# Output projection of a hybrid decoder layer by pairs of token blocks, with seven products of sums for half of the features

## The chip, the cores and the metric

The kernel runs on one core of one Trainium2 chip. The time is the device time of one execution in microseconds (us); the profile adds one execution that was recorded by the hardware profiler. TensorE is called PE here (PEld is its loading of weights), VectorE is DVE, ScalarE is ACT, GpSimd is POOL, and SP is SyncE, which only issues transfers.

## What is computed

One layer for 4096 prompt tokens and 64 sample tokens of width 1024, all in float32:

```python
h = _rmsnorm(x, g_pre)
z = h @ w_in
cb, cc, ch, cg, q, k, v, ag, mq, mg = _split_cols(z)
out_a = jax.nn.silu(cg) * cb * conv          # 256 features, conv of width 3 over cc * ch
out_b = jax.nn.silu(ag) * o_b                # 512 features, attention in a window of 128, 8 heads, 2 kv heads, sinks
out_c = jax.nn.silu(mg) * o_c                # 256 features, attention into 256 memory tokens, 4 heads
y = jnp.concatenate([out_a, out_b, out_c], axis=-1) @ w_out
return x + _rmsnorm(y, g_post), new_conv, new_k, new_v
```

The last three lines matter most here: a concatenation `mix` of 1024 features per token, its product with the 1024 x 1024 matrix `w_out`, and the normalisation of that product's rows.

## The kernel before

A float32 product is made of three matmuls on rounded parts: every operand is split into a high part (a copy in the format `F32R`) and a low part (the rest), and high x high, low x high and high x low are added in a PSUM bank. In the code these are the triples `((0, 0), (1, 0), (0, 1))`.

The program has two large stages. `input_projection` makes z for all tokens in three phases (itself with Strassen's seven products) and stores queries, keys, values and gates in DRAM buffers `qd`, `vd`, `md`; near its end it also makes the memory keys and handles the first chunk's attention. Then `open_attention` opens the pools of the second stage, which runs over 32 blocks of 128 prompt tokens; two blocks are a chunk of 256 tokens, and `NCH` is 16 chunks.

A `Block` (line 1565) is one block's output projection. `load` fetches its rows of x into `xr` (two buffers), `split` makes the high and low parts of the block's `mix`, and `run` (line 1592) goes through two halves of 512 output columns; each half accumulates 8 k-steps of 128 features, three matmuls a step, in one bank of the PSUM pool `z`, which has two. After a half, DVE multiplies the bank by the gain `gpost` into `yn` (line 1614) and ACT squares the bank in place and sums the squares (line 1615). The row factor is made on DVE and POOL (lines 1620, 1621), and `finish` (line 1629) adds the scaled `yn` to `xr` and stores the result; it is called through `finish_block` in the next block.

The attention of two blocks ahead is woven into this. `starts_of` gives for each k-step the functions that are traced ahead of its matmuls; a number in `first_at`, `memory_at` and `second_at` is a k-step counted through all blocks, 16 to a block. For each half chunk h:

- `first_half` (line 1644): transposes of the memory probabilities of the half before, window scores of this half (line 1323), the products of probabilities and values of the half before (lines 1381, 1387, 1059), its gates, and this half's softmax. This is the burst of attention in the traces.
- `memory_half`: memory scores (line 1345) and their softmax.
- `second_half`: transposes of the window's probabilities (line 1369), their masks by POOL (lines 1302, 1305), and transposes of values.

The loads come by whole chunks: `chunk_load` fetches keys (`kst`, 384 positions, four DMAs from POOL's queue, line 1088), values and queries (`q`, six DMAs from SP's queue from chunk 2 on, line 1103); `load_mix` fetches the chunk's `mix` (three places in turn).

The order of PE's instructions is the order of the program up to block 25 (a manual schedule); from block 26 on PE, and on DVE, ACT, POOL and SP all through the second stage, the framework's scheduler sets the order when the program is built, apart from instructions pinned by `keep_in_program_order`. Each engine then goes through its own list in that order. The 64 sample tokens' attention is cut into pieces that `late` calls in blocks 26 to 30, and their output block stands between blocks 30 and 31; block 31 has its second half in two parts of 256 columns.

SBUF tiles of 4 KB a partition come from the pool `wa` of 21: 16 hold the split `w_out` (`wo[k][half]`), one holds `gpost`, four are left for the parts of `mix`.

## Time and profile before

| | |
|---|---|
| median of 3 runs | 1524.7 us (1523.94 to 1525.41) |
| profiled execution | 1525.19 us |
| its span in the trace | 1523.4 us |
| granted PE clock, mean | 0.999 |
| first output matmul starts | 929.9 us into the span |
| DMA in all | 306.31 MB |

The profile's page has, in this order, the busy time of each engine, the span in 40 slices, the DMA queues, the chain of work that ended last (followed back from the last instruction, at each step to what released it), the costliest groups of instructions, and the DMA issues. A row of a group names line, engine, operation, output and input; `x24` is the number of instructions, then come the busy time, the mean in ns of one, and after the second bar the engine's idle time just before them with what ended it. A timeline row starts with start and duration in us. A windows row has the stretch, its length, then busy time and number of instructions for PE, weight loads, DVE, ACT and POOL, the granted clock, the DMA share and GB/s. Matmuls are pipelined: a group's mean for one is longer than the distance between two.

### The profile page before, as it was taken

The page shows a single profiled execution, that of the slowest core. Times are in us where ns is not written, and L with a number is a line of the kernel's source. Part 1 is how long each engine was busy: PE and PEld are TensorE (multiplying, and loading weights), DVE is VectorE, ACT ScalarE, POOL GpSimd, SP SyncE. Part 2 cuts the span into 40 slices and gives each one's busy share as a digit, 9 for nine tenths or more (in the row PEclk, how much of TensorE's full clock was granted, in tenths as well). Part 3 has the DMA queues.
Part 4 walks back from the last instruction along what each step waited for, and adds up shares of the span by engine and source line. Part 5 has one row for each costly group of instructions (what it writes and reads, how often), then busy time and mean ns, then how long its engine had stood idle before and what let it go on. Part 6 is the DMA issues. An engine that isn't in the chain of part 4 may idle for free.

```text
span 1523.4 us, 30591 instructions
## 1 busy us (share of the span) xinstructions
PE 1511.3 (99%) x11581; PEld 1395.8 (92%) x11581; DVE 1137.1 (75%) x1965; ACT 794.3 (52%) x1949; POOL 334.3 (22%) x551
## 2 busy tenths in 40 slices
PE   9999999999999999999999999999999999999998
PEld 9999999999999999999999999888788888888877
DVE  6779887899988777896776768776666666666653
ACT  6676665575322222354454446566555555655541
POOL 0223322211300000000101302333433333444310
PEclk9999999999999999999999999999999999999999
DMA  9999999978855333578787797966665666666332
GB/s 271 165 242 228 283 287 270 267 243 297 209 182 182 127 127 115 192 230 283 237 262 242 210 304 250 272 157 169 164 150 149 156 156 162 154 150 152 129 122 97
DMA packets 178456, 306.31 MB, mean 201 GB/s; under 512 B 34438, under 2 KB 108166, under 8 KB 178278
## 3 DMA queue, kind: packets, MB, share of 16 engines
q1 hardware_dynamic: 153749, 249.41, 55.4%
q0 software_dynamic: 23840, 53.90, 14.3%
q8 instruction: 92, 1.51, 0.5%
q10 hardware_dynamic: 720, 1.05, 0.2%
q14 instruction: 55, 0.44, 0.1%
HBM read 197.23 MB, written 108.05 MB: 200 GB/s over the span
## 4 chain that ended last, share of the span: by engine, by line
PE 82%; DMA 8%; DVE 4%; issue 2%; ACT 2%; POOL 1%; SPq 0%; DVEq 0%; POOLq 0%; ACTq 0%
PE c L368 44%; PE y L1607 23%; PE ws L1323 3%; DMA nat<-in_x_p 2%; PE wo L1387 2%; PE wo L1059 2%; PE xs L1345 2%; PE xt L1357 2%; PE wt L1369 2%; PE wo L1381 1%; DMA x_0B<-in_xt 1%; DMA qd<-zh 1%; PE mem_acc L789 1%; DMA ws2A<-in_w_in 1%; DMA ws4A<-in_w_in 1%
## 5 line engine op out<-in xcount | busy, mean ns | idle before, releaser
L1607 PE MATMUL y<-wo,mh 128*128 128x512 f32 (+1 forms) x1040 | 341.6, 394 | 0.0
L375 DVE TENSOR_TENSOR z<-c,z 128x520 f32<-128x520 f32 (+1 forms) x308 | 194.6, 646 | 81.1 <-PE c L368 79.8
L1607 PEld LDWEIGHTS y<-wo,mh 128*128 128x128 f32 x1040 | 194.3, 188 | 44.2 <-issue 6.8
L1607 PE MATMUL y<-wo,ml 128*128 128x512 f32 (+1 forms) x520 | 201.8, 388 | 0.0
L1279 ACT ACTIVATE sm<-sm,wnm 128x128 f32<-128x128 f32 x256 | 99.5, 390 | 70.8 <-DVE wnm L1273 70.8
L1181 POOL TENSOR_SCALAR xp<-xp,xrd 128x256 f32<-128x256 f32 x128 | 60.5, 486 | 262.0 <-DVE xrd L1175 261.5
L1607 PEld LDWEIGHTS y<-wo,ml 128*128 128x128 f32 x520 | 97.9, 188 | 16.7
L1169 ACT ACTIVATE xp<-xs,xnm 128x256 f32<-128x256 f32 x128 | 59.1, 474 | 54.1 <-PE wt L1369 34.5
L1614 DVE TENSOR_TENSOR yn<-y,gpost 128x512 f32<-128x512 f32 (+1 forms) x66 | 45.1, 683 | 42.9 <-PE y L1607 42.5
L1305 POOL TENSOR_SCALAR_AFFINE_SELECT wpt<-wpt 128x512 f32<-128x512 f32 x64 | 59.3, 944 | 43.8 <-ACT wpt L1297 43.1
L1333 DVE COPY_PREDICATED sm<-wmask,ws 128x512 f32<-128x512 uint8 x60 | 40.6, 731 | 37.6 <-ACT sm L1332 37.6
L1088 POOL DMA_DIRECT2D kst<-qd x64 | 38.9, 624 | 105.6 <-PE ws L1323 82.7
L737 POOL CAST wmask<-negs 128x256 uint8<-128x256 f32 x1 | 1.1, 1113 | 266.9 <-DMA negs<-in_wmask 266.9
L1323 PE MATMUL ws<-kst,q 128*128 128x256 f32 (+1 forms) x480 | 55.8, 297 | 0.0
L276 ACT ACTIVATE nat<-nat 104x1024 f32<-104x1024 f32 x40 | 42.3, 1059 | 25.4 <-DMA nat<-in_x_p 25.4
L1615 ACT ACTIVATE y<-y 128x512 f32<-128x512 f32 (+1 forms) x66 | 38.2, 579 | 32.6 <-DVE yn L1614 32.6
L1361 ACT COPY xpt<-xt 128x512 f32<-128x512 f32 x30 | 17.6, 587 | 72.0 <-DVE xpt L1361 72.0
L407 ACT CAST zh<-z 128x520 fp32r<-128x520 f32 x56 | 33.4, 625 | 36.5 <-DVE z L375 32.4
L1323 PEld LDWEIGHTS ws<-kst,q 128*128 128x128 f32 (+1 forms) x480 | 46.5, 187 | 4.1
L377 ACT COPY z<-c 128x520 f32<-128x520 f32 (+1 forms) x44 | 24.4, 554 | 48.8 <-PE c L368 44.6
L1279 ACT ACTIVATION_READ_ACCUMULATOR sm<-sm,wnm 128x1 f32 x256 | 48.1, 188 | 0.0
L1629 DVE SCALAR_TENSOR_TENSOR xr<-yn,yst,xr 128x1024 f32<-128x1024 f32 (+2 forms) x34 | 43.1, 1269 | 5.6 <-POOL yst L1621 4.1
(973 smaller groups left out, 5069.8 us busy)
## 6 DMA issues: line engine op xcount, KB each, us to landing
q<-qd SPq DMA_DIRECT2D x84, 256.0 KB
xr<-in_x_p SPq DMA_DIRECT2D x32, 512.0 KB
nat<-in_x_p SPq DMA_DIRECT2D x39, 416.0 KB
o_yp<-xr SPq DMA_DIRECT2D x31, 512.0 KB
md<-th POOLq DMA_DIRECT2D x48, 260.0 KB, 6.4
qd<-zh SPq DMA_DIRECT2D x48, 260.0 KB
qd<-z SPq DMA_DIRECT2D x48, 260.0 KB
kst<-qd POOLq DMA_DIRECT2D x60, 192.0 KB, 4.1
```

Source lines behind the costliest of these rows:

```text
L276: S.activation(t[:RG], t[:RG], AF.Square, accum_out=r[:RG, i : i + 1])
L368: TE.matmul(bank[:, :HW], l, r, start=first and i == 0, stop=last and i == 3 * KH - 1)
L375: add = lambda dst, other: V.tensor_tensor(dst, c, other, op=ALU.add)
L1169: S.activation(p[:, i, :], s[:, i, :], AF.Exp, bias=nm[:, i : i + 1], scale=SCALE, accum_out=den[:, i : i + 1])
L1181: G.tensor_scalar(p[:, i, :], p[:, i, :], self.rds[h][:, i : i + 1], 0.5, op0=ALU.mult, op1=ALU.mult)
L1279: S.activation(sm[:, hh, :], sm[:, hh, :], AF.Exp, bias=nm[:, hh : hh + 1], scale=SCALE, accum_out=den[:, hh : hh + 1])
L1305: G.affine_select(p3, p3, pattern=[[0, 4], [1, P]], compare_op=ALU.is_ge, fill=0.0, base=0, channel_multiplier=-1)
L1323: TE.matmul(out(kvh, col, bank), q(kvh, col, bank)[r], k(kvh, part)[r], start=first, stop=True, skip_group_check=not first, **place)
L1333: V.copy_predicated(sm4, third["wmask"].unsqueeze(1).to_broadcast([P, 2, 2, P]), s4[:, :, :, 0:P])
L1607: TE.matmul(acc, self.hl[l][:, k], wo[k][c0 // 512][:, r, c0 % 512 : c0 % 512 + c1 - c0], start=j == 0, stop=j == passes * KT - 1)
L1614: V.tensor_tensor(yn[:m, c0:c1], acc[:m], gpost[:m, c0:c1], op=ALU.mult)
L1629: x = V.scalar_tensor_tensor(self.xr[:m, cs], yn[:m, cs], st[:m, 3:4], self.xr[:m, cs], op0=ALU.mult, op1=ALU.add)
```

## The change

Blocks 0 to 5 (chunks 0 to 2) go as before. From chunk 3 on, the two blocks of a chunk are one `Pair`. Its `mix` has 256 tokens and 1024 features; for the first 512 features (convolution and memory) tokens and features are cut in two, and the columns of `w_out` too, so that four products of quarters become Strassen's seven products of sums. The other 512 features (window attention) stay plain. The seven use five sums of parts of `w_out`, T1, T3, T4, T6 and T7, made once during the first six blocks (`weight_sum`; T6 and T7 go to DRAM and back, into slots of `wo` that are free by then), and for each pair four sums of parts of `mix`, made on POOL and split by ACT and DVE. Two accumulators are read in the middle of their sums (`s3`, `s4` and the differences), and later sums are added outside PSUM. The order of the products is that of `run`.

A pair has 30 k-steps; where the attention's functions stand changes with it. Queries and keys are loaded by half chunks (`half_load`, traced in `second_half`), keys with 256 positions for each half, and from chunk 2 on both from SP's queue. `mix` has two places instead of three, and `yn` two buffers instead of one. The memory probabilities' transposes are copied back into their own tile. The memory keys and values have tiles of their own. The sample block uses T3 and T4 too, 32 matmuls as before, and is run inside the last pair, whose last quarter is made in two halves of 256 columns. PE's manual order ends before chunk 13, as before at block 26.

```diff
-        vp = ctx.enter_context(tc.tile_pool(name="vp", bufs=5, side="right"))
+        vp = ctx.enter_context(tc.tile_pool(name="vp", bufs=4, side="right"))
...
+        wt = att.enter_context(tc.tile_pool(name="wt", bufs=6))
+        places = {tag: att.enter_context(tc.tile_pool(name=tag, bufs=2)) for tag in ("sm", "p", "yn", "pt", "pv")}
+        sums = {tag: att.enter_context(tc.tile_pool(name=tag, bufs=1)) for tag in ("s3", "s4", "sum")}
...
+        def load_keys(self, i):
+            t = self.t0 + i * P
+            pool = bp["k"] if i else third["pre"]
+            self.ks[i] = pool.tile([P, 4, P + CT] if i == 0 else [P, 4, CT], F32R, tag="k", name=f"kst{self.c}_{i}")[:, :, :CT]
+            self.fill_keys(G if self.c == 1 else DMA, self.ks[i], t - P, CT)
...
+        def load_queries(self, i):
+            self.q[i] = third["pre"].tile([P, 12, P], F32R, tag="q", name=f"q{self.c}_{i}", bufs=2)
...
-                pt = work([P, 2, CT], "xpt", f"xpt{c}_{2 * i + j}")
+                pt = self.xps[j]
...
+    class Pair:
+        def lows(self, t, src):
+            S.copy(t[:, 0], src)
+            V.tensor_tensor(t[:, 1], src, f(t[:, 0]), op=ALU.subtract)
...
+        def sums_of(self, raw, t, *terms):
+            raw = raw[:, : t.shape[2] * P].rearrange("p (b n) -> p b n", n=P)
+            n = t.shape[2] // len(terms)
+            for i, (x, y, op) in enumerate(terms):
+                G.tensor_tensor(raw[:, n * i : n * i + n], x, y, op=op)
+            self.lows(t, raw)
...
+            def product(acc, a, ws, new, cs=left_):
+                for k, w in enumerate(ws):
+                    if cs.start == 0:
+                        starts.get(at[0], lambda: None)()
+                        at[0] += 1
+                    for i, (l, r) in enumerate(((0, 0), (1, 0), (0, 1))):
+                        first = new and k + i == 0
+                        TE.matmul(acc, a[:, l, k], w[:, r, cs], start=first, stop=k == len(ws) - 1 and i == 2, skip_group_check=not new)
...
+            def done(n, p, acc):
+                cs = (left_, right_)[p]
+                V.tensor_tensor(y[n][:, cs], acc, gpost[:, cs], op=ALU.mult)
+                square(n, p, acc, acc)
+            def added(n, p, acc, s, junk, cs=None):
+                cs = cs or (left_, right_)[p]
+                V.tensor_tensor(y[n][:, cs], acc, s, op=ALU.add)
+                if n == 1:
+                    finish_block(True)
+                square(n, p, y[n][:, cs], junk)
+                self.blocks[n].factor(st[n])
+                G.tensor_tensor(y[n][:, cs], y[n][:, cs], gpost[:, cs], op=ALU.mult)
...
+            c12, c21 = psum("z", f"y{c}_c12"), psum("z", f"y{c}_c21")
+            product(c12, self.a11, t["T3"], True)
+            S.copy(s3, c12)
+            product(c21, self.a22, t["T4"], True)
+            S.copy(s4, c21)
+            product(c12, self.rows[0], b22, False)
+            V.tensor_tensor(y[0][:, left_], s3, c12, op=ALU.subtract)
+            G.tensor_tensor(y[0][:, left_], y[0][:, left_], s4, op=ALU.add)
+            product(c21, self.rows[1], b11, False)
+            less = sums["sum"].tile([P, 512], F32, tag="sum", name=f"less{c}")
+            V.tensor_tensor(less, s4, c21, op=ALU.subtract)
+            G.tensor_tensor(s3, s3, less, op=ALU.add)
+            product(c12, self.w[0], plain(1, range(4, 8)), False)
+            done(0, 1, c12)
+            product(c21, self.w[1], plain(0, (4, 5)), False)
+            c11 = psum("z", f"y{c}_c11")
+            product(c11, self.diagonal, t["T1"], True)
+            V.tensor_tensor(s3, s3, c11, op=ALU.add)
+            product(c21, self.w[1][:, :, 2:4], plain(0, (6, 7)), False)
+            done(1, 0, c21)
+            product(c11, self.down[1], t["T7"], False)
+            product(c11, self.w[0], plain(0, range(4, 8)), False)
+            added(0, 0, c11, y[0][:, left_], s4)
+            ends(0)
+            if not last:
+                c22 = psum("z", f"y{c}_c22")
+                product(c22, self.down[0], t["T6"], True)
+                product(c22, self.w[1], plain(1, range(4, 8)), False)
+                added(1, 1, c22, s3, s4)
+                ends(1)
+                return
...
+    def weight_sum(o, k):
+        t = wt.tile([P, 2, 512], F32R, tag="w", name=f"wt{o}{k}")
+        raw = [sums[tag].tile([P, 512], F32, tag=tag, name=f"w{tag}{o}{k}") for tag in ("s3", "s4")]
+        for r, (kk, h) in zip(raw, (x, y)):
+            DMA.dma_start(r, a["w_out"][kk + k][:, 512 * h : 512 * h + 512])
+        G.tensor_tensor(raw[0], raw[0], raw[1], op=op)
...
+    PLAIN_PAIRS = 3
+    start_of = lambda c: 32 * c if c < PLAIN_PAIRS else 32 * PLAIN_PAIRS + 30 * (c - PLAIN_PAIRS)
...
+    first_at = {2: 4, 3: 20, 4: 34, 5: 48, 6: 62, 7: 76, 8: 90}
+    first_at |= {h: start_of((h - 3) // 2) + 8 + 15 * ((h - 3) % 2) for h in range(9, 2 * NCH + 1)}
+    memory_at = {h: n + (7 if h == 2 else 5) for h, n in first_at.items()}
+    second_at = {h: n + (12 if h == 2 else 9 if h > 9 and h % 2 == 0 else 8) for h, n in first_at.items()}
...
+        at(e - 10, p.plain_parts)
+        at(e - 3, p.row_sums)
+        at(e - 2, lambda p=p: p.window_parts(0))
+        at(e + 2, lambda p=p: p.window_parts(1))
+        at(e + 4, p.diagonal_sum)
+        at(e + 8, p.column_differences)
+        at(start_of(c - 1) + 6, p.load)
```

In the names of the steps, step n of a pair is the n-th of its 30 k-steps: T3 has 0 and 1, T4 2 and 3, b22 4 and 5, b11 6 and 7, the window's part of c12 8 to 11, of c21 12, 13, 16 and 17, T1 14 and 15, T7 18 and 19, the window's part of c11 20 to 23, T6 24 and 25, and the window's part of c22 26 to 29.

361 lines of the change are left out of this document (235 added, 126 removed).

## The prediction

> **What bounds the kernel now.** I read the page's first part first, then its chain of waits, then the chain in order of time over two blocks in the middle of the output stage, then busy times of that stage.
>
> ```profile
> span 1523.4 us, 30591 instructions
> PE 1511.3 (99%) x11581; PEld 1395.8 (92%) x11581; DVE 1137.1 (75%) x1965; ACT 794.3 (52%) x1949; POOL 334.3 (22%) x551
> PE c L368 44%; PE y L1607 23%; PE ws L1323 3%; DMA nat<-in_x_p 2%; PE wo L1387 2%; PE wo L1059 2%; PE xs L1345 2%; PE xt L1357 2%; PE wt L1369 2%; PE wo L1381 1%; DMA x_0B<-in_xt 1%; DMA qd<-zh 1%; PE mem_acc L789 1%; DMA ws2A<-in_w_in 1%; DMA ws4A<-in_w_in 1%
> ```
>
> The profiled execution took 1525.2 us, 1.8 beside its span, 0.5 above the median of the runs shown (1524.7). PE is busy throughout, but a busy PE need not be a full one, so the chain in order of time decides (start, length, what):
>
> ```profile
> 1204.19 5.49 PE y L1607 x24
> 1209.68 0.87 PE xt L1357 x8
> 1210.55 1.62 PE ws L1323 x15
> ...
> 1214.65 4.30 PE y L1607 x18
> 1218.95 0.95 PE xs L1345 x8
> 1219.90 1.39 PE y L1607 x6
> 1221.29 0.87 PE wt L1369 x8
> 1222.16 0.22 PE vtp L1681 x2
> 1222.38 5.50 PE y L1607 x24
> ```
>
> Every piece is PE's, one behind the other: this stage lasts as long as its matmuls take to issue. 24 output matmuls take 5.49 us, 0.229 us each (the 389 ns of one in the groups include overlap). The block from 1204.19 to 1222.38 has 18.2 us: 48 x 0.229 = 11.0 of output and 7.2 of attention, 5.0 of it in one burst (1209.68 to 1214.65). The other engines have room here (PE clock 1.00, DMA share 0.61):
>
> ```profile
> 1100.00:1300.00 200.00, 200.00 (x1338) 164.81 (x1337) 134.88 (x310) 115.69 (x410) 77.30 (x122) 1.00 0.61 151
> 1199.31 0.34 SPq L1632 DMA_DIRECT2D o_yp<-xr  x1
> 1235.47 0.34 SPq L1632 DMA_DIRECT2D o_yp<-xr  x1
> ```
>
> (The stores are two rows of SP's timeline.) Columns of the first row: window, sum, then PE, weight load, DVE, ACT, POOL, clock, DMA. The two stores lie two blocks apart: 36.2 us. In these DVE works 134.88/200 x 36.2 = 24.4 us, ACT 20.9, POOL 14.0.
>
> **What the change removes.** Two blocks now cost 2 x 16 k-steps of three matmuls, 96. Counted from the calls of `product`, a pair costs seven products of two k-steps (42 matmuls; T3, T4, b22, b11, T1, T7, T6) and the window's sixteen k-steps left plain (48), 90. Thirteen pairs save 13 x 6 = 78 matmuls of 512 columns, 78 x 0.229 = **17.9 us**. The attention's matmuls stay as many, the sample block's 32 too. So 17.9 is all there can be; the rest is what is given back.
>
> **The load on the other engines, per pair.**
>
> ```profile
> L1332 ACT COPY sm<-ws 128x512 f32<-128x512 f32 x22 | 11.8, 589 | 0.8
> L1287 DVE TENSOR_TENSOR sm<-sm,wrd 128x512 f32<-128x512 f32 x22 | 15.2, 692 | 0.8
> L1614 DVE TENSOR_TENSOR yn<-y,gpost 128x512 f32<-128x512 f32 x22 | 15.1, 688 | 15.9 <-PE y L1607 15.9
> L1589 DVE TENSOR_TENSOR ml<-mix,mh 128x1024 fp32r<-128x1024 f32 x8 | 12.2, 1530 | 1.8 <-ACT mh L1588 1.8
> L1588 ACT CAST mh<-mix 128x1024 fp32r<-128x1024 f32 x7 | 7.4, 1054 | 1.9 <-PE y L1607 1.9
> L1398 DVE TENSOR_TENSOR mix<-mix,wo 128x256 f32<-128x256 f32 x7 | 2.9, 414 | 0.0
> ```
>
> DVE loses two L1589 (3.1) and four L1614 (2.8). It gains four 512-column and three 256-column low parts and seven 512-column operations on accumulators: 11 x 0.69 + 3 x 0.41 = 8.8. Net 2.9: 27.3 us in a pair of 36.2 - 1.4 = 34.8, 78%. ACT loses 2 x 1.05 and gains six 512-column copies (four parts, s3, s4) and three of half size: 6 x 0.59 + 3 x 0.4 - 2.1 = 2.6, to 23.5 (68%). POOL has no two-input operation of this width now; its sums, adds and gains by gpost come to 512 + 256 + 512 + 512 + 512 + 1024 = 3328 columns a pair.
>
> ```profile
> L1302 POOL TENSOR_SCALAR_AFFINE_SELECT wpv<-wpt x62: 627/636/1620, 850.1 to 1462.0; 128x512 f32<-128x512 f32 x62
> L468 POOL TENSOR_TENSOR cacc<-cacc,z x4: 323/388/460, 391.7 to 397.5; 128x64 f32<-128x64 f32 x4
> L1088 POOL DMA_DIRECT2D kst<-qd x20 | 12.1, 620 | 11.9 <-PE ws L1323 10.3 <-issue 1.6
> ```
>
> (Shortest, median and longest in the first two rows.) Bounds: one-input masks of 512 columns at a median of 636 ns (1.24 ns a column, 4.1 us a pair) and the narrow two-input add at 388 ns for 64 (6.1 ns a column, mostly its start, 20.2 us). I take 2.5 ns, twice the lower since two tensors are read: 8.3 us. The key loads' issues leave POOL (4 x 0.62): 14.0 - 2.5 + 8.3 = 19.8, 57%. No engine passes PE by its sum; what counts is when each hands over. [...]
>
> **The hand-overs, where PE can now wait.** There are two accumulators (`z`). Today 24 matmuls lie between the end of one use and the next need of its bank. In a pair the places are: step 4 needs s3's copy of c12 (steps 2, 3 between: 6 matmuls, 1.4 us, and a value/mask turn); step 6 needs s4 (1.4 us); step 8 needs y0's subtraction (1.4 us and a burst); step 12 needs `less`; step 14 takes c12's bank for c11, after `done` (gain on DVE, then square on ACT); step 18 needs s3's addition. ACT's copy takes 0.59 and DVE's operation 0.69, so a free engine keeps all of these. The tight one is step 14, as the same work is placed today at the same distance behind a burst:
>
> ```profile
> 1217.21 0.62 PE L1607 MATMUL y<-wo,mh 128*128 128x512 f32 x2
> 1218.38 0.68 DVE L1614 TENSOR_TENSOR yn<-y,gpost 128x512 f32<-128x512 f32 x1
> 1219.10 0.58 ACT L1615 ACTIVATE y<-y 128x512 f32<-128x512 f32 x1 [0.49 <-DVE yn L1614]
> ```
>
> The bank's last matmul ended by about 1217.4, DVE came 1.0 us later, because it was still in the softmax that follows the burst, and ACT let the bank go at 1219.7: 2.3 us. In a pair steps 12 and 13 (1.4 us) and the memory scores (0.95) lie between: 2.3 us. Nothing hides what comes on top. Lower bound 0. Upper bound: two of the new 0.69 operations (a low part, an addition) stand ahead, 1.4 us, and 0.2 of semaphores: 1.6 us a pair. I take 0.3 us, near the lower row, since `less`, y0 and the low parts fall due before or in the burst, in which DVE is mostly idle: 13 x 0.3 = **3.9 us** (0 to 21). Behind T1's waiting matmul stand the second half's transposes, for which ACT's mask copies and POOL's masks wait.
>
> From the memory scores at step 28 to step 6 of the next pair ACT has three part copies, s3, s4 and a square, 6 x 0.59 = 3.5 us, beside the exponentials and mask copies that it has there today, in eight steps (5.5 us) and the memory and value turns (0.95 + 0.87 + 0.22). It is full there, and a copy that stands one place too low costs its 0.59: I take **0.5 us** in all, 0 to 8 (0.6 a pair), near the lower end since the 1.4 us between use and use cover two such places.
>
> The masks on POOL follow the second half's transposes, and the next burst needs them:
>
> ```profile
> 1206.63 1.22 POOL L1302 TENSOR_SCALAR_AFFINE_SELECT wpv<-wpt 128x512 f32<-128x512 f32 x2
> 1207.81 2.20 POOL L1305 TENSOR_SCALAR_AFFINE_SELECT wpt<-wpt 128x512 f32<-128x512 f32 x2
> ...
> 1212.10 0.43 PE L1381 MATMUL wo<-wpv,vt 64*64 64x256 f32 x2
> ```
>
> They are done at 1210.0, needed at 1212.1: 2.1 us spare. The second half moves two steps closer to the burst (six instead of eight, 1.4 us), but the memory half moves as far ahead of it. Between them POOL gets the diagonal sum (256 columns, 0.6 us, in its idle time) and y0's addition (1.3): 0, with 2.1 us as cover.
>
> **Loads.** Keys go from POOL's queue to SP's, as eight loads a chunk instead of four and 2 x 256 positions instead of 384; queries as twelve of 512-byte rows instead of six of 1024.
>
> ```profile
> q1 hardware_dynamic: 18095, 26.10, 49.0%
> SPq L1632 <- DVE wden L1284: 181.7, 20, 14.0
> L1103 SPq DMA_DIRECT2D q<-qd x83: 573/611/746, 945.4 to 1386.7; - x83
> DMA to landing us min/median/max: 3.4/4.1/10.8
> ```
>
> (Queue totals of the same 200 us; SP's waits from 1000 to 1500: sum, times, longest; issue of the queries; landing of the keys.) A packet takes 0.49 x 16 x 200 / 18095 = 87 ns. A pair adds 1536 packets of queries and 512 of keys: at most 2048 x 87 ns / 16 = 11 us on each DMA engine, at least the bytes alone (0.25 MB, 1.7 us at 151 GB/s). The share goes from 0.61 to between 0.68 and 0.95. A half's ten issues take 6.1 us, landing 4.1 (the keys' row), and an output store waiting for DVE holds SP for 181.7/20 = 9.1 us: 19.3 in sum. From the second half in which the load is issued to the burst that reads it are 22 steps (15.1 us) and some 7 of attention: 22. Covered, by little; I take 0, upper end below.
>
> **First chunks and the end.** Ten weight sums, each two loads of 256 KB, one operation on POOL, ACT and DVE, and T6, T7 out and back, come while DMA is full:
>
> ```profile
> 940.00:960.00 20.00, 20.00 (x135) 16.55 (x135) 14.36 (x37) 12.98 (x52) 7.18 (x13) 1.00 1.12 282
> ...
> 1511.77 0.28 PE L1607 MATMUL y<-wo,ml 128*128 128x256 f32 x1
> ...
> 1517.29 0.28 PE L1607 MATMUL y<-wo,mh 128*128 128x256 f32 x1
> 1517.60 0.37 ACT L1615 ACTIVATE sq<-y 128x256 f32<-128x256 f32 x1 [1.88 <-PE y L1607]
> 1519.06 1.41 DVE L1629 SCALAR_TENSOR_TENSOR xr<-yn,yst,xr 128x512 f32<-128x512 f32 x2 [0.41 <-POOL yst L1621]
> ```
>
> (First the stretch from 940, with the columns of the window above and a DMA share of 1.12; then the timeline of the end.) PE runs unhindered in the stretch even so, and half chunks ask for less ahead: **0.6 us**, 0 to 5. At the end both kernels have matmuls of 256 columns, and 48 of them take 5.5 us, 0.115 each, half of 0.229: nothing. Behind the last one an addition of 256 columns (0.41) now precedes the square: **0.5 us**.
>
> Sum: 1525.2 - 17.9 + 3.9 + 0.5 + 0.6 + 0.5 = 1512.8 for the profiled execution, 1512.3 for the median. With the lower ends 1507; with all of the likely middle 1519.
>
> **The rivals.** *The banks eat it.* At 17.4/13 = 1.3 us of waiting a pair nothing is left. For it: DVE at 78% and a 2.3 us release against 2.3 us. Against: elsewhere in the pair bursts cover. At 1.3 us: 1525.2 - 17.9 + 16.9 + 1.6 - 0.5 = 1525.3.
>
> *Keys late on SP: slower.* For it: holds up to 14.0 us and landings to 10.8 make 30.9 against 22, 9 us late; POOL's own queue had no such hold. It decides from 3 us beyond the usual 19.3. If one half in three of 26 is 4 us late, some 9 x 4 = 36: 1548. Against: the waiting stores belong to steps 29 and 8, three steps and more ahead of the loads at 2 and 16.
>
> *POOL and DVE keep each other out.* The 636 ns mask takes up to 1620, L1589 spreads from 1215 to 1755 ns where both run. If each added operation is so blocked, by 1.0 us, diagonal sum and y0 take 0.6 + 1.3 + 2.0 = 3.9 ahead of the masks, 1.8 beyond the spare 2.1, in each pair: 23 us, 1535. The break-even is 3.5 us of POOL ahead of the masks.
>
> ```profile
> L1589 DVE TENSOR_TENSOR ml<-mix,mh x20: 1217/1500/1755, 958.3 to 1444.3; 128x1024 fp32r<-128x1024 f32 x20
> ```
>
> [...]
>
> *It doesn't do what it says*: the period is set elsewhere and PE only looks full. Then 1524.7. The chain speaks against it.
>
> **Chances.** Forecast 0.68 (its own range 1507 to 1519), banks 0.14, keys 0.07, POOL 0.08, nothing 0.03. What a measurement can tell from no change is about 0.2%, 3.0 us. Faster, under 1521.7: 0.68 and 0.05 of the banks, 0.73. Within: 0.06 of the banks and 0.03, 0.09. Slower: 0.07 + 0.08 + 0.03, 0.18. From 1506.5 to 1528 lie the forecast but for 0.02 and the banks but for 0.02, and nothing: 0.81.
>
> **What would show it.** In the profile after: 78 fewer matmuls, output matmuls 0.229 us apart; pairs some 35.1 us apart; gaps before T1's matmuls of a few tenths, none before the masks' consumers; DVE near 78%. It is wrong if PE waits over 1.3 us a pair, for DVE or ACT at T1 (banks), for a DMA at the window scores (keys), for POOL at the masks' products.

## The result, and the profile after

The changed kernel is slower: median 1574.3 us of four runs (1572.2 to 1577.4) against 1525.1 of the kernel before on the same chip, a ratio of 1.032 (95% interval 1.028 to 1.035). The forecast was 1512.3 with a range up to 1528. The profiled execution took 1572.2 us.

The first part of the page after the change, with the columns of before:

```profile
span 1570.3 us, 30978 instructions
PE 1518.9 (97%) x11497; PEld 1384.7 (88%) x11497; DVE 1195.0 (76%) x2083; ACT 825.7 (53%) x2051; POOL 453.0 (29%) x625
```

PE has fewer matmuls and is no longer busy all the time. To see where the 46.9 us of longer span arose, I took the start of the first output matmul and that of block 6, which begins the first pair. Before the change, from PE's timeline:

```profile
930.02 0.39 PE L1607 MATMUL y<-wo,mh 128*128 128x512 f32 x1
...
1043.04 0.62 PE L1607 MATMUL y<-wo,mh 128*128 128x512 f32 x2
```

The second row is the last matmul of block 5 and, 0.23 us behind it, the first of block 6, at 1043.27. After the change the first output matmul starts at 927.42, and the first pair with

```profile
1060.03 1.54 PE L1730 MATMUL y_c<-wtT,pa 128*128 128x512 f32 x6
```

In the pairs, two stores of SP's timeline lie one pair apart; the windows row covers nine pairs (window, its length, PE, weight load, DVE, ACT, POOL, clock, DMA share, GB/s):

```profile
1116.41 0.34 SPq L1656 DMA_DIRECT2D o_yp<-xr  x1
...
1154.53 0.34 SPq L1656 DMA_DIRECT2D o_yp<-xr  x1
1116.41:1459.51 343.10, 324.37 (x2125) 256.75 (x2125) 250.15 (x578) 205.53 (x731) 187.65 (x234) 1.00 0.56 156
```

| part of the span | before | after | change |
|---|---|---|---|
| up to the first output matmul | 930.0 | 927.4 | -2.6 |
| the six plain blocks | 113.3 | 132.6 | +19.4 |
| 13 pairs, by the distance of two blocks | 13 x 36.2 | 13 x 38.1 | +25.5 |
| the rest (way into the first pair, last pairs, sample) | | | +4.6 |

The first row says nothing of the change: in the profiles of the runs below, which all make z by the same code, the first output matmul starts between 927.2 and 934.7.

Two blocks became 2.0 us longer where 1.1 us less was forecast, and the six blocks that stay plain lost 19 us. None of PE's helpers is full in the pairs: of 343.10 us DVE works 73%, ACT 60%, POOL 55%. The losses are waits at hand-overs.

**A pair's five waits.** PE's timeline at T1 of one pair, and from the end of that pair into the next:

```profile
1194.57 0.86 PE L1730 MATMUL y_c<-wo,pw 128*128 128x512 f32 x3
1195.92 1.64 PE L1730 MATMUL y_c<-wtT,pd 128*128 128x512 f32 x6 [0.48 <-ACT y_c L1733]
...
1214.08 1.54 PE L1730 MATMUL y_c<-wtT,pa 128*128 128x512 f32 x6
...
1216.33 0.38 PE L1883 MATMUL vtp<-ident,vT 128*128 128x128 f32 x2
1216.96 1.67 PE L1730 MATMUL y_c<-wtT,pa 128*128 128x512 f32 x6 [0.25 <-DVE yn L1742]
1218.80 3.44 PE L1730 MATMUL y_c<-wo,pr 128*128 128x512 f32 x12 [0.17 <-ACT s L1756]
1222.08 1.03 PE L1365 MATMUL xt<-ident,xp 128*128 128x128 f32 x8
...
1225.68 0.43 PE L1389 MATMUL wo<-wpv,vt 64*64 64x256 f32 x2 [0.96 <-ACT xp L1369]
```

The bracket shows only the part of a wait in which PE's array stood idle, so I took the distances: a matmul issues in 0.229 us, six in 1.37. T1 (step 14) starts 1195.92 - 1194.57 - 3 x 0.229 = 0.66 us late. T4 (step 2) starts some 0.4 late behind the two transposes. T4's six end at 1218.33, and b22 starts at 1218.80, 0.47 late (step 4). The twelve of b22 and b11 need 2.75 and take 3.28, 0.53 late (step 6). The values' products wait 0.96 (step 8). That is 3.0 of the 3.3 us by which a pair, 38.1 us, is longer than the 34.8 of its PE work.

Who is late at steps 4 and 8, from the timelines of the others:

```profile
1217.14 2.31 POOL L1190 TENSOR_SCALAR xp<-xp,xrd 128x256 f32<-128x256 f32 x2 [1.78 <-DVE xrd L1184]
1217.54 0.64 ACT L1733 ACTIVATE s<-yn 128x512 f32<-128x512 f32 x1
1218.15 0.59 ACT L1756 COPY s<-y_c 128x512 f32<-128x512 f32 x1
1219.42 1.28 POOL L1747 TENSOR_TENSOR yn<-yn,gpost 128x512 f32<-128x512 f32 x1
1220.68 0.93 POOL L1190 TENSOR_SCALAR xp<-xp,xrd 128x256 f32<-128x256 f32 x2
1222.11 0.72 POOL L1686 TENSOR_TENSOR yn<-mix 128x256 f32<-128x256 f32 x1
1222.78 1.43 POOL L1310 TENSOR_SCALAR_AFFINE_SELECT wpv<-wpt 128x512 f32<-128x512 f32 x2
1222.86 0.41 ACT L1671 CAST pd<-yn 128x256 fp32r<-128x256 f32 x1 [2.33 <-POOL yn L1686]
...
1224.17 1.22 POOL L1313 TENSOR_SCALAR_AFFINE_SELECT wpt<-wpt 128x512 f32<-128x512 f32 x2
...
1224.95 0.58 ACT L1369 COPY xp<-xt 128x512 f32<-128x512 f32 x1 [1.69 <-DVE xp L1369]
```

T3's six matmuls, from 1214.08, had ended by 1215.45, but ACT copies c12 into s3 only at 1218.15, 2.7 us later: the exponentials of the memory scores and the squares of the quarter before (L1733) stand ahead. At step 8 the bracket names ACT's copy, which ended at 1225.53; POOL's masks ended at 1225.39. Both are late for one reason that the row of `pd` shows: the gain by `gpost` (L1747), the second factor and the diagonal sum stand ahead of the masks on POOL, and ACT stands 2.33 us in front of the rounding of that diagonal sum, DVE 2.05 us in front of its low part, with their copies of the transposes behind.

**The six blocks.** PE's waits in them (sum, times, longest), and four of the thirteen stretches of 10 us, with the columns of the windows row above:

```profile
PE xt L1365 <- POOL xp L1190: 4.6, 4, 2.3
PE wt L1377 <- DVE sm L1295: 3.0, 2, 1.9
PE wo L1389 <- ACT xp L1369: 1.5, 1, 1.5
PE xt L1365 <- ACT xp L1178: 1.3, 2, 1.0
PE wo L1389 <- POOL wpt L1313: 0.2, 1, 0.2
```

```profile
940.00:950.00 10.00, 7.21 (x37) 5.25 (x35) 2.75 (x9) 4.55 (x15) 4.28 (x7) 0.93 1.02 231
950.00:960.00 10.00, 10.00 (x74) 8.14 (x74) 7.36 (x17) 5.89 (x23) 2.14 (x4) 0.90 0.83 239
...
980.00:990.00 10.00, 6.95 (x24) 5.42 (x23) 4.71 (x13) 5.26 (x21) 5.83 (x9) 0.66 0.94 309
...
1010.00:1020.00 10.00, 8.50 (x59) 6.23 (x58) 6.36 (x16) 5.83 (x23) 2.81 (x3) 0.83 0.80 233
```

The waits are 10.6 us. The clock is 1.00 in the nine other stretches; in these four it falls short of full speed by 10 x (0.07 + 0.10 + 0.34 + 0.17) = 6.8 us. Of these 0.6 lie within a wait (1.2 us at a clock of 0.50, from 982.80), so some 6 us came on top of the waits, by this estimate. How the first wait comes about, from the timelines of POOL, ACT and PE:

```profile
945.72 1.26 POOL L1815 TENSOR_TENSOR ws3T<-ws3T,ws4T 128x512 f32<-128x512 f32 x1 [5.77 <-DMA ws3T<-in_w_out]
946.97 2.27 POOL L1190 TENSOR_SCALAR xp<-xp,xrd 128x256 f32<-128x256 f32 x4
947.01 0.63 ACT L1817 ACTIVATE wtT<-ws3T 128x512 fp32r<-128x512 f32 x1 [4.25 <-POOL ws3T L1815]
947.49 1.00 PE L1365 MATMUL xt<-ident,xp 128*128 128x128 f32 x4 [2.32 <-POOL xp L1190]
```

POOL's next instruction is a weight sum whose operands have not landed. It stands there for 5.77 us, ACT for 4.25 in front of that sum's rounding, and the memory factors that PE's transposes need (L1190) stand behind it.

### The profile page after: what moved, and what is told of

The parts are those of the page before. It is cut to its first block, busy times and chain, and to the rows that moved or that the text cites. A ratio compares the mean times of both kernels' runs of the same rounds, so it can differ in the third digit from the quotient of the medians.

```text
span 1570.3 us, 30978 instructions
## 1 busy us (share of the span) xinstructions
PE 1518.9 (97%) x11497; PEld 1384.7 (88%) x11497; DVE 1195.0 (76%) x2083; ACT 825.7 (53%) x2051; POOL 453.0 (29%) x625
## 3 DMA queue, kind: packets, MB, share of 16 engines
q8 instruction: 91, 1.49, 0.4%
## 5 line engine op out<-in xcount | busy, mean ns | idle before, releaser
L1730 PE MATMUL y_c<-wo,pw 128*128 128x512 f32 (+1 forms) x636 | 161.6, 393 | 0.0
L1730 PEld LDWEIGHTS y_c<-wo,pw 128*128 128x128 f32 x636 | 113.3, 188 | 24.5 <-issue 3.9
L1190 POOL TENSOR_SCALAR xp<-xp,xrd 128x256 f32<-128x256 f32 x128 | 76.4, 612 | 108.2 <-DVE xrd L1184 108.2
L1178 ACT ACTIVATE xp<-xs,xnm 128x256 f32<-128x256 f32 x128 | 58.9, 471 | 20.8 <-DVE xmx L1169 11.0
L1636 PE MATMUL y<-wo,mh 128*128 128x512 f32 x192 | 65.9, 407 | 0.0
L1313 POOL TENSOR_SCALAR_AFFINE_SELECT wpt<-wpt 128x512 f32<-128x512 f32 x64 | 44.0, 705 | 38.2 <-ACT wpt L1305 37.9
L1295 DVE TENSOR_TENSOR sm<-sm,wrd 128x512 f32<-128x512 f32 x64 | 53.4, 834 | 1.6
L1369 ACT COPY xp<-xt 128x512 f32<-128x512 f32 x30 | 17.6, 586 | 67.2 <-DVE xp L1369 67.2
L377 ACT COPY z<-c 128x520 f32<-128x520 f32 (+1 forms) x44 | 24.4, 554 | 52.7 <-PE c L368 46.8
L1730 PE MATMUL y_c<-wtT,pa 128*128 128x512 f32 x156 | 43.2, 412 | 4.9 <-DVE yn L1742 2.9
L1310 POOL TENSOR_SCALAR_AFFINE_SELECT wpv<-wpt 128x512 f32<-128x512 f32 x62 | 41.9, 698 | 17.0 <-ACT wpt L1305 17.0
L1747 POOL TENSOR_TENSOR yn<-yn,gpost 128x512 f32<-128x512 f32 x25 | 35.7, 1430 | 38.5 <-ACT s L1733 38.5
L1730 PE MATMUL y_c<-wo,pr 128*128 128x512 f32 x156 | 42.6, 410 | 3.2 <-ACT s L1756 2.0
```

The costliest lines, as they stand in the source:

```text
L1178: S.activation(p[:, i, :], s[:, i, :], AF.Exp, bias=nm[:, i : i + 1], scale=SCALE, accum_out=den[:, i : i + 1])
L1190: G.tensor_scalar(p[:, i, :], p[:, i, :], self.rds[h][:, i : i + 1], 0.5, op0=ALU.mult, op1=ALU.mult)
L1295: V.tensor_tensor(sm, sm, rd.unsqueeze(2).to_broadcast([P, 4, P]), op=ALU.mult)
L1310: G.affine_select(pv.rearrange("p (h q) -> p h q", h=4), p3, pattern=[[0, 4], [-1, P]], compare_op=ALU.is_gt, fill=0.0, base=0, channel_mu ...
L1313: G.affine_select(p3, p3, pattern=[[0, 4], [1, P]], compare_op=ALU.is_ge, fill=0.0, base=0, channel_multiplier=-1)
L1636: TE.matmul(acc, self.hl[l][:, k], wo[k][p][:, r], start=k + i == 0, stop=k + i == KT + 1)
```

## The experiments

Eighteen kernels ran, all made from the changed kernel. The six blocks are measured from the first output matmul to the first pair's (in e9 to the end of their last matmul), a pair by every second store over eight or nine pairs. Each is read from one profile: the changed kernel, e3, e4, e7 and e8 have the same six blocks and took 131.2 to 132.7 us, so a difference under some 2 us says nothing. The ratio is to the kernel before on the same chip, with its 95% interval.

| run | six blocks, us | pair, us | median, us | ratio |
|---|---|---|---|---|
| the changed kernel | 132.6 | 38.1 | 1574.3 | 1.032 (1.028 to 1.035) |
| e1_no_sums | 111.8 | 38.2 | 1557.7 | 1.020 (1.016 to 1.023) |
| e2_early_operands | 132.4 | 38.2 | 1576.7 | 1.031 (1.028 to 1.035) |
| e3_gain_dve | 132.7 | 37.4 | 1567.0 | 1.025 (1.022 to 1.029) |
| e4_squares_aside | 131.3 | 38.1 | 1573.0 | 1.029 (1.026 to 1.032) |
| e5_sums_spread | 132.1 | 38.1 | 1576.2 | 1.034 (1.032 to 1.037) |
| e6_window_parts_later | 133.6 | 37.5 | 1567.7 | 1.028 (1.026 to 1.030) |
| e7_release_by_copy | 131.5 | 37.0 | 1560.9 | 1.024 (1.022 to 1.026) |
| e8_memory_early | 131.2 | 43.0 | 1617.2 | 1.061 (1.058 to 1.064) |
| e9_traffic_only | 111.9 | 38.2 | 1564.8 | 1.025 (1.023 to 1.026) |
| e10_sums_no_operands | 123.8 | 38.2 | 1567.1 | 1.026 (1.024 to 1.028) |
| e11_row_sums_early | 130.6 | 37.0 | 1564.0 | 1.025 (1.022 to 1.027) |
| e12_sums_in_sbuf | 139.4 | 37.0 | 1569.4 | 1.028 (1.026 to 1.029) |
| e13_stages_apart | 133.1 | 38.1 | 1579.8 | 1.035 (1.032 to 1.038) |
| e14_s3_on_dve | 133.6 | 36.6 | 1557.8 | 1.021 (1.019 to 1.023) |
| e15_all_mended | 131.9 | 36.6 | 1557.2 | 1.020 (1.016 to 1.024) |
| e16_sums_in_gaps | 128.7 | 38.1 | 1573.3 | 1.030 (1.027 to 1.033) |
| e17_gaps_and_pairs | 129.2 | 36.6 | 1552.2 | 1.016 (1.013 to 1.018) |
| e18_gaps_no_operands | 125.4 | 38.1 | 1565.8 | 1.025 (1.022 to 1.028) |

### The six blocks: are the weight sums the price?

```diff
-            at(10 + 16 * n + 6 * k, lambda o=o, k=k: weight_sum(o, k))
+            at(10 + 16 * n + 6 * k, lambda o=o, k=k: third["wt"][o].__setitem__(k, {"T1": wo[2 + k][0], "T3": wo[2 + k][1], "T4": wo[k][0]}.get(o)))
...
-        DMA.dma_start(f(t), f(td[o][k]))
```

> This kernel leaves out the ten weight sums of the first chunks, with their loads, stores and reloads: the products T1, T3, T4, T6 and T7 use plain tiles of the output weights in their place, so the first two columns of the output are other sums than the reference's; every matmul stays. Theory (the weight sums hold the POOL queue while their operands land, the factors of the memory attention stand behind them, PE waits, and after each wait the clock is low for some us): the six plain blocks take 113 us as before instead of 132.8, the granted clock there is 1.0, and the time falls by about 20 us to 1554; the pairs stay at 38.1 us. Rival (the half-chunk loads with their two buffers are late, whatever the sums do): the six blocks stay above 127 us and the time falls by under 6 us, to 1568 or more.

Two of the worst stretches in this run:

```profile
940.00:950.00 10.00, 10.00 (x62) 8.76 (x60) 5.77 (x20) 7.00 (x30) 4.54 (x9) 1.00 0.94 310
...
980.00:990.00 10.00, 9.99 (x79) 7.94 (x77) 6.45 (x16) 6.34 (x24) 4.00 (x8) 1.00 0.98 244
```

PE is full and its clock 1.00, at much the same DMA share. The sums cost these blocks 132.6 - 111.8 = 20.8 us, all that they had lost (19.4) and a little more; the half-chunk loads, which are still there, cost nothing. The span fell by 17.2 us, since the output stage began 3.2 us later in this run. The next runs take the sums apart: their transfers, their operands' lateness, their work.

```diff
 # e9_traffic_only
-        t = wt.tile([P, 2, 512], F32R, tag="w", name=f"wt{o}{k}")
+        t = {"T1": wo[2 + k][0], "T3": wo[2 + k][1], "T4": wo[k][0], "T6": wo[2 + k][0], "T7": wo[2 + k][0]}[o]
...
-        G.tensor_tensor(raw[0], raw[0], raw[1], op=op)
...
-            S.copy(t[:, 0], raw[0])
-            V.tensor_tensor(t[:, 1], raw[0], f(t[:, 0]), op=ALU.subtract)
 # e10_sums_no_operands
-            DMA.dma_start(r, a["w_out"][kk + k][:, 512 * h : 512 * h + 512])
-        G.tensor_tensor(raw[0], raw[0], raw[1], op=op)
+        G.tensor_tensor(raw[0], gpost[:, :512], gpost[:, 512:], op=op)
```

> This kernel leaves out the ten weight sums themselves (POOL's add, ACT's rounding, DVE's remainder) and keeps every one of their transfers: the operand loads, the four stores and the four reloads, which carry plain tiles instead; the first two columns of the output are other sums than the reference's. Theory A (transfers: the operands' 5.2 MB come while the DMA engines are 0.75 to 1.0 busy, and SP's queue holds queries and keys behind them; that would explain why neither early operands nor spread sums gained): the six blocks stay above 127 us, the time above 1568. Theory B (engine queues: POOL stands in front of a sum whose operands have not landed): nothing waits for the loads any more, the six blocks take 112 to 115 us, the time is 1553 to 1557. Anything between is shared.

> This kernel leaves out the operand loads of the ten weight sums: POOL adds the two halves of the output gain instead, and the rounding, the remainder, the stores and the reloads stay, so that all engine work of the sums is there and none of it waits for an operand; the first two columns of the output are other sums than the reference's. Theory A (transfers) and theory B (POOL held by late operands) both give 112 to 116 us for the six blocks and 1553 to 1559 in all. Rival (the engine work itself, 1.28 us of POOL, 0.6 of ACT and 0.68 of DVE each, put into queues that are just in time): the six blocks stay above 125 us and the time above 1566.

With the traffic alone the six blocks take 111.9 us, to the end of their last matmul at 1042.87. (The time is above the forecast because T3's stand-in is a tile that T6's reload fills, so the first pair waits 7.4 us for it.) Theory A falls. With the work alone they take 123.8: the engine work costs 12.0 us without any operand to wait for, and what late operands add is, by difference, the other 132.6 - 123.8 = 8.8. Theory B and the rival both hold, for 8.8 and 12.0. How work costs PE time, in e10's timelines:

```profile
950.89 1.26 POOL L1813 TENSOR_TENSOR ws3T<-gpost 128x512 f32<-128x512 f32 x1
952.19 0.62 ACT L1818 CAST wtT<-ws3T 128x512 fp32r<-128x512 f32 x1 [4.42 <-POOL ws3T L1813]
952.71 0.58 ACT L1369 COPY xp<-xt 128x512 f32<-128x512 f32 x1
...
953.39 0.43 PE L1389 MATMUL wo<-wpv,vt 64*64 64x256 f32 x2 [3.25 <-issue]
```

POOL comes to the add only behind its masks; ACT stands 4.42 us in front of the rounding, the copy that PE needs is behind, and PE waits 3.25.

Three ways to let the sums pass unnoticed, all computing everything:

```diff
 # e2_early_operands: weight_terms is the two loads of weight_sum
+            at(4 + 16 * n + 8 * k, lambda o=o, k=k: weight_terms(o, k))
+            at(10 + 16 * n + 8 * k, lambda o=o, k=k: weight_sum(o, k))
 # e5_sums_spread: both operands in one tile of the pool wa
+            at(24 + 12 * n + 6 * k, lambda o=o, k=k: weight_terms(o, k))
+            at(34 + 12 * n + 6 * k, lambda o=o, k=k: weight_sum(o, k))
 # e13_stages_apart: loads, POOL's add, ACT's rounding, DVE's remainder
+            for d, fn in ((0, weight_terms), (5, weight_add), (8, weight_high), (10, weight_low)):
+                at(10 + 16 * n + 8 * k + d, lambda o=o, k=k, fn=fn: fn(o, k))
```

> All computed. The operands of a weight sum are loaded six steps (some 7 us) before the sum is queued on POOL, instead of with it. Theory (a queue held by a wait, not a shortage of the DMA engines): POOL no longer waits 5.8 us at the sums, the memory factors are in time, and most of the 20 us comes back: the six blocks take 113 to 120 us and the time is 1555 to 1562. Rival (the loads of the sums, 512 KB each pair, and the half-chunk loads fill the DMA engines, so that operands or queries land late anyway): the six blocks stay above 127 us and the time above 1568.

> All computed. Each weight sum gets a tile of its own for its two operands, loaded ten steps (some 12 us) before the sum; the sums start at step 34 instead of 10 and follow each other every six steps up to step 88, so that no load waits for the sum before it, and none lies among the stores and loads of the first block. Theory (queues held by a wait: in e2_early_operands the next loads still stood behind the sum before, because the two operand tiles are single, and SP's queue stood behind them): POOL and SP wait for no operand, the six blocks take 112 to 118 us instead of 132.8, the time is 1554 to 1560. Rival (the sums' own work on POOL, DVE and ACT, 2.6 us each, or their bytes are the price, wherever they stand): the six blocks stay above 125 us, the time above 1566.

> All computed; against the changed kernel only the weight sums differ: the four stages of a sum (operand loads, POOL's add, ACT's rounding, DVE's remainder) are queued at steps 0, 5, 8 and 10 of its turn instead of all at once, and a sum follows the one before after eight steps; the work is the same. Theory (a chain through three in-order queues: ACT and DVE stand in front of a stage whose predecessor has not begun, and the softmax and the copies for PE stand behind them): the six blocks take 113 to 119 us instead of 132.6, and the time is 1554 to 1561. Rival (the work itself, 26 us over three engines just in time, costs the 12 us of e10): the six blocks take 124 us or more, the time is 1565 or more.

All three missed: 132.4, 132.1 and 133.1 us. In e2 the two operand tiles are single, so a load waits on SP for the sum before it, with queries and keys behind, and POOL still stands in front of its adds, 10.5 us at the longest. In e5 the loads wait on SP for a slot of `wa` that PE has still to leave (sum, times, longest):

```profile
SPq L1815 <- PE y L1636: 13.4, 3, 6.1
```

In e13 an add stands between two masks on POOL (967.91), and ACT and DVE wait 1.66 and 2.07 us in front of their stages.

In e1 POOL is idle for 9 to 12 us at a time up to 1009 us, mostly between the masks and the next factors, and for 2 to 7 us at a time behind that; two runs put the sums behind the masks, two behind each of five first halves, and a third took them from the parts in SBUF:

```diff
 # e16_sums_in_gaps (operands in tiles of wa); e18_gaps_no_operands the same without the loads
+            for d, fn in ((-9, weight_terms), (1, weight_add), (4, weight_high), (5, weight_low)):
+                at((20, 34, 48, 62, 76)[n] + 2 * k + d, lambda o=o, k=k, fn=fn: fn(o, k))
 # e12_sums_in_sbuf (on top of e11): r = 0 four and r = 1 two steps ahead of the rest
+        G.tensor_tensor(t, f(wo[kx + k][hx][:, r]), f(wo[ky + k][hy][:, r]), op=op)
...
+        V.tensor_tensor(raw[0], raw[0], raw[1], op=ALU.add)
```

> All computed; e11_row_sums_early, and the weight sums are made of the high and low parts of the output weights that lie in SBUF (two adds on POOL, one on DVE each) instead of operands loaded from DRAM: no operand loads, 13 us more of POOL and 7 us of DVE over the six blocks. If late operands or their transfers are the price of the sums (theories A and B of e9_traffic_only), the six blocks take 114 to 120 us and the time is 1530 to 1540; if it is the engine work itself, the six blocks take 130 us or more and the time is that of e11_row_sums_early or above.

> All computed; against the changed kernel only the weight sums differ. Two sums follow the first half of each of five half chunks (steps 20, 34, 48, 62, 76): operands loaded ten steps earlier into a tile of their own, POOL's adds one and three steps behind that half, where POOL is idle for 9 to 12 us in e1_no_sums, the rounding and the remainder three and four steps later still. Theory (where the sums stand in the queues decides, not their work): the six blocks take 113 to 119 us against 132.6 in the changed kernel and 123.8 with no operands in e10, and the time is 1554 to 1562. Rival (work and bytes cost the same anywhere): 124 us or more, the time 1565 or more.

> This kernel leaves out the operand loads of the weight sums, as e10_sums_no_operands does (POOL adds the two halves of the output gain), and puts the sums where e16_sums_in_gaps has them, two behind each of five half chunks; the first two columns of the output are other sums than the reference's. In e10 the ten adds ran in one dense row from 941 to 981 us and cost PE 12 us there, and nothing after it. Theory (the place of a sum in the queues decides): with the adds in POOL's idle stretches and no operand to wait for, the six blocks take 111.8 to 116 us, and the time is 1552 to 1558. Rival (the work of the sums costs PE the same anywhere): 121 us or more, the time 1563 or more. Between: both.

e12 is a miss that teaches most: no operand is loaded at all, POOL and DVE work 20 us more by its forecast, and the blocks take 139.4, 8.8 us more than e11, on which it is built and which has the loads. e16 gains 3.9 us on the changed kernel, e18 another 3.3 and stays 13.6 above e1. In e16 POOL still waits for operands (4.13 us at its first add), ACT 4.89 and DVE 6.23 for the stages behind it. So the theory of place falls as I put it: the work of the sums costs 12 to 14 us of PE in both orders tried, on engines that are 40 to 70% busy over the stage. PE's timelines of e16 and e1 show it place by place. From burst to burst, by the memory values' products (L1059), e16 takes 24.4, 19.1, 19.0, 19.2 and 18.8 us and e1 16.6 to 16.9: the first two sums, with their late operands and a low clock behind (0.83 from 960 to 970 us), cost 7.7 us, and each later two 2.2 to 2.4, whether POOL's adds ran in its idle time (975 to 1000 us) or right ahead of and among the factors (1022 to 1026, 1042 to 1047). At some 1.1 us a sum that is 11 for ten, near e10's 12.0. My reading, which no run shows by itself, is that the chains to PE (softmax to transposes, factors to transposes, masks to products) have no slack of the size of a sum's stage, and that each of the three stages goes into one of them. Whether a place exists that is free, and how much of the 12 is the stage itself and how much the queue standing in front of it, stays open.

### The pairs: which queue holds which hand-over?

```diff
 # e3_gain_dve, in added()
-                G.tensor_tensor(y[n][:, cs], y[n][:, cs], gpost[:, cs], op=ALU.mult)
+                V.tensor_tensor(y[n][:, cs], y[n][:, cs], gpost[:, cs], op=ALU.mult)
```

> All computed. The product with the output gain behind the last sums of a pair's blocks goes from POOL to DVE. Theory (at step 8 the attention's values wait about 1.0 us for POOL's masks, which stand behind this product of 1.28 us): the wait for the masks goes, a pair takes 37.1 us instead of 38.1, and 13 pairs give 13 us: 1561. Rival 1 (the profile's releaser of that wait is right: ACT's copy of the cross-attention's shares is the late one): pairs stay at 38.0 to 38.2 and the time within 3 us of 1574. Rival 2 (DVE, late at steps 2 and 4 already, takes the loss over): pairs at 38.1 or more, the time 1574 to 1584.

A pair takes 37.4 us, 0.7 less. None of PE's waits from 1116 to 1440 is for the values' products now; the one that grew is T4's (sum, times, longest):

```profile
PE y_c L1730 <- DVE yn L1742: 4.2, 9, 0.5
```

The wait at step 8 is gone, although its bracket had named ACT: POOL's queue was its cause. A fifth of it came back at step 2, where DVE is now later (0.5 us each against 0.3), so rival 2 has a small part.

```diff
 # e4_squares_aside, in done()
-                square(n, p, acc, acc)
+                square(n, p, acc, s4)
 # e7_release_by_copy (with e3), in done() for c12
+                V.tensor_copy(y[n][:, cs], acc)
+                square(n, p, y[n][:, cs], s4)
+                V.tensor_tensor(y[n][:, cs], y[n][:, cs], gpost[:, cs], op=ALU.mult)
```

> All computed. The squares of the second and third finished quarter write to the tile s4 in place of the bank itself, so that DVE's gain and ACT's squares can read the bank side by side. Theory (T1 at step 14 waits 0.65 us because the bank is given back only after 0.68 us of DVE and then 0.67 us of ACT): that wait falls to 0.1 to 0.3 us, a pair takes 37.6 to 37.8 us, and the time falls by 4 to 6 us to 1568 to 1570. Rival (ACT or DVE comes to the bank late for other work and the order of the two matters little): pairs stay at 38.0 or more and the time at 1572 to 1576.

> All computed; with the gain on DVE as in e3_gain_dve. The bank of c12 is given back by one plain copy on DVE; the squares and the gain then read that copy in SBUF. (In e4_squares_aside ACT still began only when DVE's gain had ended, at 1194.32 against 1194.22 us, so the two reads of one bank never ran side by side.) Theory (T1's wait of 0.6 us at step 14 is the second read of the bank): the wait goes, a pair takes 36.8 to 37.0 us against 37.45, the time is 1558 to 1561. Rival (the added 0.68 us of DVE a pair makes DVE late elsewhere, at steps 2 and 16): pairs at 37.3 us or more and the time 1565 or more.

e4 changed nothing, 38.1 us. DVE's gain and ACT's squares in its timeline:

```profile
1193.54 0.68 DVE L1737 TENSOR_TENSOR yn<-y_c,gpost 128x512 f32<-128x512 f32 x1
...
1194.32 0.60 ACT L1733 ACTIVATE s<-y_c 128x512 f32<-128x512 f32 x1 [0.59 <-DVE wden L1292]
```

ACT idles 0.59 us and starts 0.10 us after DVE's gain has ended, though the two now only read the bank. (The bracket names a small DVE instruction behind the gain, on which the squares don't depend.) In this pair, then, the bank is held by two reads in a row; why ACT doesn't start earlier, the trace doesn't show. e7, which has only one, gains 0.46 us a pair (37.44 to 36.98): T1, by distances some 0.7 us late in e3, is 0.01 to 0.07 late, and a part of that came back elsewhere.

```diff
 # e6_window_parts_later (with e3)
-        at(e - 2, lambda p=p: p.window_parts(0))
-        at(e + 2, lambda p=p: p.window_parts(1))
+        at(e + 3, lambda p=p: p.window_parts(0))
+        at(e + 6, lambda p=p: p.window_parts(1))
 # e8_memory_early (with e3): five steps behind the first half become three
+    memory_at = {h: n + (7 if h == 2 else 5 if h < 9 else 3) for h, n in first_at.items()}
 # e11_row_sums_early (with e3, e6, e7)
-        at(e - 3, p.row_sums)
+        at(e - 9, p.row_sums)
 # e14_s3_on_dve (with e3, e6, e7)
-            S.copy(s3, c12)
+            V.tensor_copy(s3, c12)
```

> All computed; with the gain on DVE as in e3_gain_dve. The splits of the window attention's two blocks into high and low parts are moved from steps -2 and 2 to steps 3 and 6 (they are needed at steps 8 and 12). Theory (the hand-overs at steps 2, 4 and 6 are late because DVE and ACT are behind with these splits of 0.68 and 0.62 us each when the bank's add and the copies s3 and s4 fall due): these three waits, some 1.3 us a pair together, fall to 0.5 or less, a pair takes 36.3 to 36.8 us against 37.45 in e3_gain_dve, and the time is 1552 to 1559. Rival (the softmax of the memory scores alone keeps DVE and ACT late, or the moved splits make the products of steps 8 and 12 late): pairs at 37.3 us or more, the time 1565 or more.

> All computed; with the gain on DVE as in e3_gain_dve. The memory scores of a half chunk are put three steps behind its first half instead of five, so that their maxima and exponentials come 1.4 us earlier, ahead of the hand-overs at steps 2, 4 and 6 and not among them. Theory (the exponentials, 1.8 us of ACT in a row, are what the copies s3 and s4 stand behind): the three waits fall from some 1.3 us a pair to 0.6 or less, a pair takes 36.6 to 37.0 us against 37.45, the time is 1555 to 1561. Rival (DVE and ACT are then still busy with the window softmax, so the exponentials start no earlier, and the transposed shares at step 16 or 2 come late): pairs at 37.4 us or more, the time 1566 or more.

> All computed; with the gain on DVE (e3_gain_dve), the release by a copy (e7_release_by_copy) and the window parts later (e6_window_parts_later), and now also the row sums put at step -9 instead of -3. In e6_window_parts_later the wait at step 2 went and the one at step 4 grew from 0.17 to 0.9 us, with the same 37.45 us a pair, so the copy s3 is what comes last: it stands on ACT behind four exponentials that start when DVE has taken the maxima. Theory (DVE's and ACT's splitting of the row sums, 0.68 and 0.6 us, holds the maxima and the exponentials up): they start earlier, the copy comes in time, and a pair takes 35.6 to 36.3 us against 36.98 in e7_release_by_copy; the time is 1545 to 1552. Rival (the exponentials and the squares of the last quarter, 2.6 and 0.8 us in a row on ACT, are too long whenever they start): a pair takes 36.8 us or more, the time is 1558 or more.

> All computed; with the gain on DVE, the release of c12 by a copy and the window parts later (as in e11_row_sums_early, without its move of the row sums), and the snapshot s3 of step 2 copied by DVE instead of ACT. Theory (the wait at step 4 is ACT's queue: the copy stands behind four exponentials and the squares of the last quarter): it falls from 0.9 us to 0.2 or less, a pair takes 35.8 to 36.3 us against 36.98 in e7_release_by_copy, and the time is 1548 to 1554. Rival (DVE is as late as ACT there): a pair takes 36.8 us or more, the time is 1558 or more.

e6: 37.5 us, no gain. The wait at step 2 went, and the one at step 4 took its place:

```profile
PE y_c L1730 <- ACT s L1756: 7.1, 8, 0.9
```

T4's bank was not what set the pace; the copy s3 behind it on ACT was. e8 is far off, 43.0 us a pair: steps 2 to 6 wait less, but ACT's squares of c12 now come behind the exponentials of memory scores that stand right ahead of T1, and PE waits 4.1 us there. e11 took the row sums ahead of the second block's gates, which stand at step -7: in it (and in e12) that block's memory features are summed before they are gated, so that the second block of each pair comes out as other sums than the reference's. Its pair took 36.97 us against 36.98 in e7: the rival, that the exponentials and squares are too long whenever DVE lets them start, holds. e14 takes the copy off ACT, and the pair falls to 36.6, a smaller gain than forecast (35.8 to 36.3). What is left of it at step 4, in DVE's and PE's timelines:

```profile
1174.37 1.28 DVE L1653 SCALAR_TENSOR_TENSOR xr<-yn,yst,xr 128x1024 f32<-128x1024 f32 x1
1175.64 0.67 DVE L1761 COPY s<-y_c 128x512 f32<-128x512 f32 x1
1176.45 1.63 PE L1730 MATMUL y_c<-wo,pr 128*128 128x512 f32 x6 [0.35 <-ACT s L1733]
```

The copy, which b22 needs, ended at 1176.31 (the bracket names ACT's squares, which end about then and which b22 doesn't need). It now stands behind the final addition of a block, 1.28 us on DVE, for which nothing waits soon.

### Put together

e15 joins e13, e14 and a release by copy for block 5's last quarter (T4 of the first pair waited 2.07 us for that bank); e17 has the sums of e16 in place of e13's.

> All computed; e13_stages_apart and e14_s3_on_dve together, and the last quarter of the sixth block gives its bank back by a copy as c12 does (T4 of the first pair waited 2.1 us for it, with a low clock behind). If the savings add up (some 15 us in the six blocks, 25 in the pairs, 3 at the entry), the time is 1529 to 1540; a pair stays at 36.2 us or more, against 36.17 for two blocks before, unless the waits left at steps 2 to 6 go, so that it does not beat the kernel before by more than a few us if at all.

> All computed; e16_sums_in_gaps with the four edits of the pairs and the entry (gain on DVE, c12 and the sixth block's last quarter released by a copy, window parts later, s3 copied by DVE). If e16's theory holds, the six blocks take 113 to 119 us, a pair 36.6 us as in e14_s3_on_dve, and the time is 1536 to 1545: still above the 1525 of before, since a pair of 36.6 us is longer than the 36.17 of two plain blocks. If it falls, the time is that of e15_all_mended, 1553 to 1560.

In e15 the blocks stayed at 131.9 us, as in e13, so it is no better than e14. e17 is the fastest that ran: 1552.2 us, still 1.6% above the kernel before (1.3 to 1.8). With 36.6 us a pair is longer than two plain blocks (36.2), and the six blocks stay 16 us longer than before on top. Of the 1.8 us by which the pair exceeds its PE work, 1.1 still lie at steps 4 and 6: b22 starts 0.64 us late behind T4's six matmuls, b11 0.47 late behind b22's. To reach the forecast the two parts would have to be nearly free of waits, some 35.1 us a pair and 113 for the six blocks.

## Why the prediction was wrong

**The matmuls saved** came as counted (84 fewer are recorded, where the code has 78 fewer), at the unchanged 0.229 us. So did the step's own bound, that there was no more to gain. Everything else is what was given back.

**Masks on POOL, costed at nothing with 2.1 us of cover.** This step failed, by some 0.7 us a pair (e3). The prediction put the diagonal sum (0.6) and y0's addition (1.3) ahead of the masks. The addition comes behind them (1225.36). Ahead stood instead the second block's gain by `gpost`, 1.28 us, which the forecast had counted in POOL's total but given no place, and the first of two pairs of factors, 2.31 us for what takes 0.93. The row "PE waits for POOL at the masks' products", which the prediction named as its refutation, was there, and one step further as well: ACT stood in front of POOL's sum. The rival that POOL and DVE keep each other out had the place, with 1.8 us a pair where 0.7 was measured; stretched factors are in the row, but no run tells what the stretch costs by itself, and the gain that e3 moved was not in the rival's list.

**T1 at step 14, taken as 0.3 us.** Measured 0.66, inside the bounds of 0 to 1.6. The mechanism, a bank given back by DVE and then ACT, was right (e7); the size taken was half of the measured one, some 5 us of the miss. No run shows the 0.2 us of semaphores in the upper bound: at T1 ACT began 0.03 us behind DVE's gain (1195.15 to 1195.18) and PE 0.06 behind ACT (1195.86 to 1195.92).

**ACT between steps 28 and 6, taken as 0.5 us in all.** This failed by more: ACT's two copies made PE wait 0.47 + 0.53 = 1.0 us a pair at steps 4 and 6, 13 us, beyond the upper bound of 8. The text said that ACT "is full there" and then took the lower end, because 1.4 us of cover lay between use and use. Cover counts from when the engine reaches the instruction; ACT reached s3's copy 2.7 us after T3 had ended, behind four exponentials that waited for DVE's maxima. Step 2, where T4 waits 0.4 us a pair for DVE's addition on its bank, another 5 us, was not on the list of hand-overs at all.

**First chunks, taken as 0.6 us (0 to 5).** The largest single error: 20.8 us (e1). The argument was that PE ran unhindered at a DMA share of 1.12 before. That was right about transfers (e9: nothing) and said nothing of the queues that a sum passes through: late operands cost 8.8 and the engine work 12.0 (e10), with some 6 of the whole in a lower clock behind the waits.

**Keys on SP, costed at nothing.** Right: no wait of PE in the pairs names a DMA, and e1 shows the half-chunk loads free in the six blocks too. The DMA share, forecast to rise from 0.61 to 0.68 or more, fell to 0.56.

**POOL's price**, 2.5 ns a column, was right: the gain of 512 columns took a median of 1.28 to 1.29 us. DVE at 73 and ACT at 60% are below the forecast 78 and 68, in a longer pair. In us a pair that is 27.8 and 22.8, against 27.3 and 23.5: the sums of busy time were right and told nothing of the result.

In sum the pairs were off by 38.1 - 35.1 = 3.0 us each, 39 us for 13; the six blocks by 19; the way into the first pair, with its wait of 2.07 us and a clock of 0.50 behind (from 1064.72 to 1068.12 us), for which the prediction had no term, and the last pairs make up the rest.
